# A hybrid decoder trunk on one core: HGRN's four heads in one tile, and fixed places for levels, outputs, splits and the compression

## The chip, the cores and the metric

The kernel runs on one core of one Trainium2 chip. The metric is the device time of one execution in microseconds, the median of repeated runs. The core's engines are TensorE (PE; its weight loads stand apart in the profile as PEld), the vector engine (DVE), the scalar engine (ACT), GpSimd (POOL) and the queue that issues the DMAs (SP). TensorE writes only to PSUM, which the kernel uses as eight banks of 128 x 512 float32.

## The reference

Two layers on 256 tokens of width 1024. Each layer, cut to what matters here:

```python
xn = rms_norm(h, norm_mix[l]);  proj = xn @ w_in[l]             # 3352 columns
# HGRN2: 4 heads of 128, chunks; per head, with b = cumsum(log f) inside a chunk
f = lb + (1 - lb) * sigmoid(f_logit);  k = 1 - f;  q = silu(q)
A = einsum(q, k, exp(b_t - b_s)), causal;  o = A v + (q exp(b)) S
S = exp(b_last) S + (k exp(b_last - b)) v
o_hg = rms_norm(o) * silu(g)
# NSA: 8 heads of 64 in 2 groups, gates over three branches
kc, vc = silu(blocks(k) + pe @ w1) @ w2                          # 15 compressed blocks
o_cmp = softmax(q kc) vc;  o_slc, o_swa: softmax attention over selected blocks and a window
h = h + concat(o_hg, o_nsa) @ w_out[l]
xn = rms_norm(h, norm_ffn[l])
h = h + (silu(xn @ w_gate) * (xn @ w_up)) @ w_ffn_out[l]         # 2816 wide
```

With 256 tokens all four blocks of 64 are selected and the window of 512 takes in every earlier token, so the kernel computes two full causal attentions (b = 0 and 1) beside the compressed one. All is float32.

## The kernel before

**Weights.** The matrices come in 204 units of at most 128 x 1024, in the order in which they are used, through four raw buffers. Each is split into a high half (`whi`, an ACTIVATE on the scalar engine, L143) and a low half (`wlo`, a subtraction on the vector engine, L144), with six buffers each. A dense product is then three TensorE products in float32r (`mm3`, L324, which keeps a list `products` of all of them); a plain float32 product shows as two instructions in the profile.

**Order.** A planner fixes the order of every engine's instructions at build, by priorities and by its own costs; on the chip each engine works through its queue in order, with semaphores between engines. `tc.high_priority(offset=...)` raises a priority, and `after(ins, others)` keeps `ins` behind `others` in that order without a wait of its own. `HOLD` and `PACE` say behind which of the `products` an instruction is held.

**A layer.** Norm and transposes of h (`norm_T`, two halves of 128 tokens); projections B, C and A for keys, values and queries; `gates(0)`, the forget gate and q of HGRN heads 0 and 1; the compression, whose hidden layer (`phid`, L510) works on four column tiles at once, is transposed (`phT`, L516), and ends in the normed and rotated key `kcb`, transposed as `pkT` (L551); `gates(1)`; then the attention scores and outputs, the projections `hi` and `hg` of HGRN (96 products in all, listed from `begin`) and HGRN's levels, which the planner interleaves.

**Attention outputs.** In `outputs(t)` a step turns four heads of probabilities in each of two groups g (`pPT`, L662), copies them to SBUF (`PT`, L666: scalar engine for g = 0, vector engine for g = 1), and multiplies them with the values (`pO`, L673), g = 0 and g = 1 on the two column tiles of 64. Two calls of two and four steps make six steps a layer. The products of one step are emitted behind the next step's transposes, but at a high priority that lets them go ahead.

**HGRN.** The decay is built up in levels. Blocks of one token (`pd`, L758), then levels 1 to 7 that double the block: at each level small products of K and Q (`pl`, L779 and L790) fill the off-diagonal part of the blocks, and the vector engine then multiplies Q by the forget product of the earlier half, K by that of the later half, and the two halves of the forget products with each other (L801, L802, L809). Levels up to 5 are merged into `blk` by a predicated copy (L814) and copied to `AT` by GpSimd; levels 6 and 7 are copied to `AT` by the scalar engine (L824). `p8` is the product across the two chunks of 128, copied to `A01` (L832). The head products `po` (L843, L844) take `AT`, `A01` and v. All of it works on two pairs of heads (hp = 0, 1), each with tiles of its own.

**Output projection and FFN's entry.** `wo_part` multiplies the mixed heads with w_out for one half t; `residual(0)`; while t = 1 is still multiplied, `norm_T(0)` makes the FFN's input for t = 0; `residual(1)`. The FFN's first column block is done per half (`ffn_in_tok`), so that `norm_T(1)` can come between them:

```python
        last, lo = norm_T(0, gain1, *X2[:2], "b", hold=begin + HOLD[2])
        for hh in range(2):
            held = units[U["fu", 0, hh]][6]
            if held is not None:
                after(held, lo)
        state["behind"] = [last]
        residual(1, py, lo)
...
        ffn_in_tok(0, 0)
        norm_T(1, gain1, *X2[:2], "b", hold=begin + HOLD[3])
        ffn_in_tok(0, 1)
```

Here `last` is the scalar engine's last copy of the normed half, `lo` are the vector engine's subtractions for its low half, and `units[...][6]` is the split's subtraction. GpSimd computes the reciprocal root of the norm in two operations (L339, L340), and the vector engine multiplies (`xn`, L343).

Of the kernel before, what the change touches and what calls it, by code (L numbers as in the profile page):

```python
# [42 lines left out]
LEV_PRIO, BLOCK_PRIO, PACE = 250, 3000, (0, 14)  # L43
HOLD, HOLD_C = (18, 18, 16, 36), 1
# [46 lines left out]
def trunk(ctx: ExitStack, tc: tile.TileContext, x, w_in, w_out, lbl, gnorm, q_gain, k_gain,  # L91
# [23 lines left out]
    state = {"loaded": 0, "split": 0}  # L115

# [16 lines left out]
    def split_to(n):  # L133
        while state["split"] < min(n, len(units)):
            load_to(state["split"] + 1)
            u = units[state["split"]]
            a, b = u[1], u[2]
            hi = wsp.tile([128, 1024], F32R, name="whi")
            lo = wsp.tile([128, 1024], F32R, name="wlo")
            u[4] = hi[:, : a * b].rearrange("p (a b) -> p a b", b=b)  # L140
            u[5] = lo[:, : a * b].rearrange("p (a b) -> p a b", b=b)
            with tc.high_priority(offset=SPLIT_PRIO):
                after(S.activation(u[4], u[3], AF.Copy), state.pop("behind", ()))  # L143
                u[6] = V.tensor_sub(u[5], u[3], u[4].bitcast(F32))  # L144
            state["split"] += 1
# [111 lines left out]
    AT = [one.tile([128, NT, 2, 128], F32, name=f"AT{hp}") for hp in range(2)]  # L257
    for hp in range(2):
        nc.gpsimd.memset(AT[hp], 0.0)
# [69 lines left out]
    def norm_T(t, gain, xh, xl, tag, behind=(), hold=None):  # L329

        with tc.high_priority():
            ss = sm.tile([128, 4], F32, name="n_ss")
            lo = []
# [7 lines left out]
            for c in range(2):  # L341
                cs = slice(512 * c, 512 * c + 512)
                V.scalar_tensor_tensor(xn[:, cs], h[:, t, cs], ss[:, 3:4], gain[c], op0=OP.mult, op1=OP.mult)  # L343
# [17 lines left out]
    for l in range(NL):  # L361
# [20 lines left out]
        HG, FB, last_sig = [], [], []  # L382

        def gates(hp):
# [3 lines left out]
            F = wk.tile([128, 2, T], F32, name="F", bufs=2)  # L388
            K = wk.tile([128, 2, T], F32, name="K", bufs=2)
# [8 lines left out]
            Q = wk.tile([128, 2, T], F32, name="Q", bufs=2)  # L398
# [3 lines left out]
            HG.append((F, K, Q))  # L402
            FB.append(wk.tile([128, 256], F32, name="FT", bufs=2))
# [97 lines left out]

        p = bank("phid", "e")[:, :256]
        for u in range(4):
            w = w1t[u]
            for jj in range(2):
                for kv in range(2):
                    for q in range(2):
                        j = 4 * u + 2 * jj + q
                        r0 = 64 * kv + 32 * q
                        PE.matmul(p[r0:r0 + 32], flat[:, kv, j], w[:, kv, 2 * jj + q],  # L510
                                  start=(j < 2), stop=(j >= 14))
# [3 lines left out]
        for c in range(2):  # L515
            PE.matmul(p[:, c], hid[:, 128 * c:128 * c + 128], C("sel"), start=True, stop=True)  # L516
# [26 lines left out]
        rk = rstd(kcs[:32], 1, 64, "kc_rs")  # L543
# [7 lines left out]
        PE.transpose(p[:, :32], kcb[:32].rearrange("p g d -> p (g d)"), ident[:32, :32])  # L551
# [100 lines left out]
        def outputs(t):  # L652
# [3 lines left out]
            def turned(b, sb):  # L656

                pts = []
                for g in range(2):
                    p = bank("pPT", "c")  # L660
                    for hg in range(4):
                        PE.transpose(p[:, 128 * hg:128 * hg + 128],  # L662
                                     P[t, g][:, hg, b, 128 * sb:128 * sb + 128], ident)
                    pt = turn[:, len(turns) % 4]
                    turns.append(pt)
                    pts.append((pt, V.tensor_copy(pt, p) if g else S.activation(pt, p, AF.Copy)))  # L666
                return pts

            def summed(b, sb, pts):

                with tc.high_priority(offset=BLOCK_PRIO):
                    for g in range(2):
                        m = PE.matmul(po[64 * g:64 * g + 64], vtok[:, b, sb, 64 * g:64 * g + 64], pts[g][0],  # L673
                                      start=(b == 0 and sb == 0), stop=False, skip_group_check=True)
                        after(m, [q[1] for q in pts])

            held = None
            for b, sb in steps:
                pts = turned(b, sb)
                if held is not None:  # L680
                    summed(*held)
# [66 lines left out]
        with tc.high_priority(offset=LEV_PRIO):  # L748
            A01, FT, blk, decays = [], [], [], []
            blocks = [(t, i, n) for t in range(NT) for i in range(2) for n in range(4)]  # L750
            for hp in range(2):
                F, K, Q = HG[hp]
                FT.append(F.rearrange("p h t -> p (h t)"))

                p = bank("pd", "b")[:, :128].rearrange("p (b s) -> p b s", s=32)
                for t, i, n in blocks:
                    ts = slice(128 * t + 32 * n, 128 * t + 32 * n + 32)
                    PE.matmul(p[32 * n:32 * n + 32, 2 * t + i], K[:, i, ts], Q[:, i, ts], start=True, stop=True)  # L758
                decays.append(V.tensor_mul(Q, Q, F))
                bl = wk.tile([128, 4, 32], F32, name="blk", bufs=2)  # L760
                blk.append(bl)
                V.tensor_mul(bl, p, C("ident32")[:, None, :].to_broadcast([128, 4, 32]))
            for lev in range(1, 8):
                half = 1 << (lev - 1)
                n4 = 256 // half

                pl = bank("pl", "b")
                if lev < 6:
                    pl = pl[:, :128].rearrange("p (g b c) -> p g b c", g=2, c=16)
                else:  # L770
                    pl = pl[:, :4 * half].rearrange("p (g c) -> p g c", g=2)
                last = None
                with tc.high_priority(offset=BLOCK_PRIO):
                    for hp in (1, 0):
                        F, K, QF = HG[hp]
                        if lev < 6:
                            for t, i, n in blocks:
                                ts = slice(128 * t + 32 * n, 128 * t + 32 * n + 32)
                                m = PE.matmul(pl[32 * n:32 * n + 32, hp, 2 * t + i], K[:, i, ts],  # L779
                                              QF[:, i, ts].rearrange("p (n c a) -> p n c a", c=2, a=half)[:, :, 1],  # L780
                                              start=True, stop=True)
                                after(m, [last] if last else [products[begin + PACE[0] + (lev - 1) * PACE[1]]] + decays)
                                last = m
                            continue
                        for t in range(NT):
                            for n in range(64 // half):
                                for i in range(2):
                                    s0 = 128 * t + 2 * half * n
                                    r0 = 64 * n + half * i
                                    m = PE.matmul(pl[r0:r0 + half, hp, half * t:half * t + half], K[:, i, s0:s0 + half],  # L790
                                                  QF[:, i, s0 + half:s0 + 2 * half], start=True, stop=True)
                                    after(m, [last] if last else decays)
                                    last = m
                decays = []
                for hp in range(2):
                    F, K, QF = HG[hp]
                    qv = QF.rearrange("p h (n c a) -> p (h n) c a", c=2, a=half)
                    kv = K.rearrange("p h (n c a) -> p (h n) c a", c=2, a=half)
                    fv = FT[hp].rearrange("p (n c) -> p n c", c=2)
                    if lev < 7:  # L800
                        V.tensor_mul(qv[:, :, 1], qv[:, :, 1], fv[:, :, 0:1].to_broadcast([128, n4, half]))  # L801
                        decays.append(V.tensor_mul(kv[:, :, 0], kv[:, :, 0], fv[:, :, 1:2].to_broadcast([128, n4, half])))  # L802
                    else:
                        f7 = FT[hp].rearrange("p (h t c) -> p h t c", t=NT, c=2)
                        V.tensor_mul(QF[:, :, 192:256], QF[:, :, 192:256], f7[:, :, 1, 0:1].to_broadcast([128, 2, 64]))
                        V.tensor_mul(K[:, :, 0:64], K[:, :, 0:64], f7[:, :, 0, 1:2].to_broadcast([128, 2, 64]))
                    if lev < 7:
                        f2 = (FB[hp] if lev % 2 else F.rearrange("p h t -> p (h t)"))[:, :n4]
                        V.tensor_mul(f2, fv[:, :, 0], fv[:, :, 1])  # L809
                        FT[hp] = f2  # L810
                    if lev < 6:
                        lm = lev_m[:, 16 * lev - 16:16 * lev]
                        dst = blk[hp].rearrange("p b (n c a) -> p b n c a", c=2, a=half)[:, :, :, 1]
                        V.copy_predicated(dst, lm[:, None, :].to_broadcast([128, 4, 16]).rearrange("p b (n a) -> p b n a", a=half),  # L814
                                          pl[:, hp].rearrange("p b (n a) -> p b n a", a=half))
# [227 lines left out]
```

## Time and profile before

| | us |
|---|---|
| median of 3 runs | 684.99 (684.43 to 685.22) |
| the profiled execution's own time | 685.0 |
| its span, first to last instruction | 683.1 |
| TensorE busy | 667.0 |
| vector engine busy | 469.7 |
| scalar engine busy | 379.6 |
| GpSimd busy | 30.1 |

The profiled execution's own time is its span and 1.9 us around it. Busy is the time in which an engine had at least one instruction in work; TensorE's products overlap, so the durations of single products add up to more than that. Starts are counted from the first instruction.

### The profile page before, as it was taken

Reading aid. Unit: us, or ns where it says so; the run is one execution under the profiler, and the core shown is the slowest. Engines: PE = TensorE matmul, PEld = TensorE weight load, DVE = VectorE, ACT = ScalarE, POOL = GpSimd, SP = SyncE. Lnnn points to the kernel's source line nnn. Section 1 sums busy time; section 2 is a strip of 40 time slices with the busy share of each in tenths; the row PEclk is TensorE's granted clock in tenths of the full one; section 3 lists DMA queues with packets and bytes.
Section 4 is the critical chain, followed back from the end, with each engine's and each line's share of the span. In section 5 each row is a group of like instructions: output and inputs, shape, how many; then the busy total and the mean of one; then the engine's idle time right before and its main releaser. Section 6 shows DMA issues by size and latency. Waiting matters only on the chain.

```text
span 683.1 us, 11845 instructions
## 1 busy us (share of the span) xinstructions
PE 667.0 (98%) x4607; PEld 554.6 (81%) x4607; DVE 469.7 (69%) x853; ACT 379.6 (56%) x676; POOL 30.1 (4%) x72
## 2 busy tenths in 40 slices
PE   6999999999999999999999999999999999999997
PEld 3869876688888888888878897658898888888886
DVE  4879999577665556666588979858685566665552
ACT  5536778636555555555466558656555555555550
POOL 2600001001000000000010000010000000000000
PEclk9999999999999999999999999999999999999999
DMA  7798541353765665666678632404376666665521
GB/s 253 246 335 266 169 107 51 100 178 121 248 187 187 190 192 194 194 185 185 196 230 286 203 110 64 125 1 154 94 229 203 188 187 190 197 191 187 185 93 62
DMA packets 86574, 118.90 MB, mean 174 GB/s; under 512 B 5035, under 2 KB 69365, under 8 KB 86518
## 3 DMA queue, kind: packets, MB, share of 16 engines
q1 hardware_dynamic: 86518, 118.15, 56.1%
q8 instruction: 36, 0.59, 0.4%
q14 instruction: 20, 0.16, 0.1%
HBM read 117.08 MB, written 1.05 MB: 173 GB/s over the span
## 4 chain that ended last, share of the span: by engine, by line
PE 80%; DVE 8%; DMA 4%; ACT 4%; issue 2%; POOL 1%; SPq 0%; POOLq 0%; DVEq 0%; ACTq 0%
PE pgu L929 22%; PE pz L327 17%; PE pgu L932 11%; PE pt L327 9%; PE py L327 5%; DMA wraw<-in_w_in_dram 4%; DVE wlo L144 3%; PE pO L673 2%; PE pgt L327 2%; ACT whi L143 2%; PE pPT L662 2%; PE pf L327 1%; PE pxn L346 1%; PE pl L779 1%; PE pq L327 1%
## 5 line engine op out<-in xcount | busy, mean ns | idle before, releaser
L144 DVE TENSOR_TENSOR wlo<-wraw,whi 128x1024 fp32r<-128x1024 f32 (+1 forms) x204 | 244.9, 1206 | 141.7 <-ACT whi L143 140.6
L143 ACT ACTIVATE whi<-wraw 128x1024 fp32r<-128x1024 f32 (+1 forms) x204 | 212.4, 1044 | 147.1 <-PE pgu L929 43.5
L929 PE MATMUL pgu<-x,whi 128*128 128x512 f32 x640 | 174.7, 394 | 0.0
L929 PEld LDWEIGHTS pgu<-x,whi 128*128 128x128 f32 x640 | 110.7, 189 | 15.7
L327 PE MATMUL pz<-whi,ahl 128*128 128x512 f32 x352 | 112.5, 391 | 0.0
L932 PEld LDWEIGHTS pgu<-x,wlo 128*128 128x128 f32 x640 | 98.1, 189 | 13.5
L932 PE MATMUL pgu<-x,wlo 128*128 128x256 f32 x640 | 101.7, 281 | 0.0
L327 PE MATMUL pt<-whi,x 128*128 128x512 f32 (+1 forms) x320 | 97.9, 383 | 0.0
L327 PEld LDWEIGHTS pz<-whi,ahl 128*128 128x128 f32 x352 | 65.9, 188 | 13.9 <-DVE ahl L946 0.5
L327 PE MATMUL pz<-wlo,ahl 128*128 128x512 f32 x176 | 68.9, 392 | 0.0
L327 PEld LDWEIGHTS pt<-whi,x 128*128 128x128 f32 x320 | 58.5, 191 | 10.3 <-DVE x L352 0.5
L327 PE MATMUL pt<-wlo,x 128*128 128x512 f32 (+1 forms) x160 | 61.6, 385 | 0.3 <-DVE wlo L144 0.3
L327 PE MATMUL py<-whi,x 128*128 128x512 f32 x128 | 42.0, 398 | 0.0
L327 PEld LDWEIGHTS pz<-wlo,ahl 128*128 128x128 f32 x176 | 33.0, 188 | 6.4
L327 PEld LDWEIGHTS pt<-wlo,x 128*128 128x128 f32 x160 | 30.6, 191 | 5.2 <-DVE wlo L144 0.7
L592 ACT ACTIVATE P<-pS,nm 128x128 f32<-128x128 f32 (+1 forms) x64 | 26.1, 424 | 6.3 <-DVE nm L639 5.0
L327 PEld LDWEIGHTS py<-whi,x 128*128 128x128 f32 x128 | 24.1, 188 | 4.7
L938 ACT ACTIVATE sl<-sl 128x512 f32<-128x512 f32 x20 | 12.7, 634 | 27.0 <-DVE sl L937 27.0
L327 PE MATMUL py<-wlo,x 128*128 128x512 f32 x64 | 25.1, 392 | 0.0
L327 PE MATMUL pf<-x,whi 128*128 128x256 f32 x128 | 23.8, 286 | 0.1
L327 PE MATMUL pgt<-whi,x 128*128 128x256 f32 x128 | 23.8, 285 | 0.0
L327 PE MATMUL pq<-x,whi 128*128 128x256 f32 x128 | 23.6, 284 | 0.0
(222 smaller groups left out, 829.4 us busy)
## 6 DMA issues: line engine op xcount, KB each, us to landing
wraw<-in_w_ffn_in_dram SPq DMA_DIRECT2D x88, 512.0 KB, 3.6
wraw<-in_w_in_dram SPq DMA_DIRECT2D x48, 512.0 KB, 5.3
wraw<-in_w_ffn_out_dram SPq DMA_DIRECT2D x44, 512.0 KB, 3.7
w<-in_cmp_w_k_dram SPq DMA_DIRECT2D x8, 512.0 KB, 4.7
w<-in_cmp_w_v_dram SPq DMA_DIRECT2D x8, 512.0 KB, 7.1
wraw<-in_w_out_dram SPq DMA_DIRECT2D x16, 256.0 KB, 4.1
wraw<-in_w_out_dram SPq DMA_DIRECT2D x8, 512.0 KB, 4.9
wraw<-in_w_in_dram SPq DMA_DIRECT2D x8, 280.0 KB, 5.3
```

Source lines behind the costliest of these rows:

```text
L143: after(S.activation(u[4], u[3], AF.Copy), state.pop("behind", ()))
L144: u[6] = V.tensor_sub(u[5], u[3], u[4].bitcast(F32))
L327: products.append(PE.matmul(o, a[u], b[v], start=start and i == 0, stop=stop and i == 2, skip_group_check=skip))
L346: tr = PE.transpose(p[:, 128 * k:128 * k + 128], xn[:, 512 * c + 128 * k:512 * c + 128 * k + 128], ident)
L592: e = S.activation(o, i, f, **kw)
L662: PE.transpose(p[:, 128 * hg:128 * hg + 128], P[t, g][:, hg, b, 128 * sb:128 * sb + 128], ident)
L673: m = PE.matmul(po[64 * g:64 * g + 64], vtok[:, b, sb, 64 * g:64 * g + 64], pts[g][0], start=(b == 0 and sb == 0), stop=False, skip_group_ ...
L779: m = PE.matmul(pl[32 * n:32 * n + 32, hp, 2 * t + i], K[:, i, ts], QF[:, i, ts].rearrange("p (n c a) -> p n c a", c=2, a=half)[:, :, 1], ...
L929: products.append(PE.matmul(pp[b], w[0][:, k, s], X[2][:, 4 * hh + k].rearrange("p c t -> p (c t)"), start=(hh == 0 and k == 0), stop=Fals ...
L932: products.append(PE.matmul(pp[b][:, T:], w[1][:, k, s], X[0][:, 4 * hh + k], start=False, stop=(hh == 1 and k == 3), skip_group_check=True))
L938: S.activation(sl, sl, AF.Silu)
```

## The change

HGRN's F, K and Q of all four heads are one tile each, and so are AT, A01, blk and FT: every level is one set of operations. The forget gate's scaling goes from the vector engine to the scalar engine. The diagonal blocks and each level are one chain of products, every level held behind a product of the projections (behind product 7 the first, then 14 further each, up to the 91st for level 7). An output's product for g = 0 stands behind the next step's transposes, that for g = 1 follows at a high priority. Compression: the hidden layer's products are one chain (in layer 1 in the order of units 3, 0, 1, 2), `phT` is held behind the 29th product of `gates(0)`, the key's reciprocal root is two GpSimd operations instead of twelve on the vector engine, and `pkT` is held behind the 8th product of `hi`. `norm_T` is cut in two: `normed` (squares, root, multiplication) and the transposes; for t = 1 `normed` is emitted right after the residual, and the weight splits around it are given fixed neighbours.

```diff
-LEV_PRIO, BLOCK_PRIO, PACE = 250, 3000, (0, 14)
-HOLD, HOLD_C = (18, 18, 16, 36), 1
+LEV_PRIO, BLOCK_PRIO, PACE = 250, 3000, (6, 14)
+HOLD, HOLD_C, HOLD_T = (18, 18, 16, 36), 1, 28
...
-                after(S.activation(u[4], u[3], AF.Copy), state.pop("behind", ()))
+                after(S.activation(u[4], u[3], AF.Copy), hi_behind.pop(0) if hi_behind else ())
                 u[6] = V.tensor_sub(u[5], u[3], u[4].bitcast(F32))
+                if lo_behind:
+                    after(u[6], lo_behind.pop(0))
+                    lo_held.append(u[6])
...
-    def norm_T(t, gain, xh, xl, tag, behind=(), hold=None):
+    def normed(t, gain, behind=()):
...
+        return xn, sq, m
+
+    def norm_T(t, gain, xh, xl, tag, behind=(), hold=None, xn=None):
+
+        if xn is None:
+            xn = normed(t, gain, behind)[0]
...
-                V.tensor_scalar(F[:, i], F[:, i], omlb[:, l, hd:hd + 1], lb[:, l, hd:hd + 1],
-                                op0=OP.mult, op1=OP.add)
+                S.activation(F[:, i], F[:, i], AF.Identity, scale=omlb[:, l, hd:hd + 1], bias=lb[:, l, hd:hd + 1])
...
+        order = (3, 0, 1, 2) if l else (0, 1, 2, 3)
+        behind = []
+        for u in order:
...
+                        with tc.high_priority(offset=BLOCK_PRIO if behind else 0):
+                            m = PE.matmul(p[r0:r0 + 32], flat[:, kv, j], w[:, kv, 2 * jj + q],
+                                          start=(u == order[0] and jj == 0), stop=(u == order[3] and jj == 1))
+                        after(m, behind)
+                        behind = [m]
...
+            m = PE.matmul(p[:, c], hid[:, 128 * c:128 * c + 128], C("sel"), start=True, stop=True)
+            after(m, [products[begin - 96 + HOLD_T]])
...
-        rk = rstd(kcs[:32], 1, 64, "kc_rs")
+        rk = sm.tile([128, 1], F32, name="kc_rs")[:32]
+        nc.gpsimd.tensor_scalar(kcs[:32], kcs[:32], 1.0 / 64, EPS, op0=OP.mult, op1=OP.add)
+        nc.gpsimd.tensor_tensor(rk, kcs[:32], mhalf[:32], op=OP.pow)
...
-            def summed(b, sb, pts):
-
-                with tc.high_priority(offset=BLOCK_PRIO):
-                    for g in range(2):
+            def summed(b, sb, pts, behind=[]):
+
+                for g in range(2):
+                    with tc.high_priority(offset=BLOCK_PRIO * g):
...
-                        after(m, [q[1] for q in pts])
+                        after(m, [q[1] for q in pts] + behind)
...
-                    summed(*held)
+                    summed(*held, behind=turned.last)
...
+        after(kT, [products[begin + 7]])
...
+                for hd in (3, 2, 1, 0):
+                    for t in range(NT):
+                        for n in range(4):
+                            m = PE.matmul(p[32 * n:32 * n + 32, 4 * t + hd], KH[:, hd, rows(t, n)],
+                                          QH[:, hd, rows(t, n)], start=True, stop=True)
+                            after(m, behind)
+                            behind = [m]
...
+                behind = [products[begin + min(PACE[0] + (lev - 1) * PACE[1], 95)], decay]
+                with tc.high_priority(offset=BLOCK_PRIO):
+                    for o, a, b in prods:
+                        m = PE.matmul(o, a, b, start=True, stop=True)
+                        after(m, behind)
+                        behind = [m]
...
+                    V.tensor_mul(qv[:, :, 1], qv[:, :, 1], fv[:, :, 0:1].to_broadcast([128, n4, half]))
+                    decay = V.tensor_mul(kv[:, :, 0], kv[:, :, 0], fv[:, :, 1:2].to_broadcast([128, n4, half]))
+                    FT = (FB if lev % 2 else FA)[:, :n4]
+                    V.tensor_mul(FT, fv[:, :, 0], fv[:, :, 1])
...
-        last, lo = norm_T(0, gain1, *X2[:2], "b", hold=begin + HOLD[2])
-        for hh in range(2):
-            held = units[U["fu", 0, hh]][6]
-            if held is not None:
-                after(held, lo)
-        state["behind"] = [last]
+        xn0, _, turn0 = normed(0, gain1)
+        last, lo = norm_T(0, gain1, *X2[:2], "b", hold=begin + HOLD[2], xn=xn0)
         residual(1, py, lo)
+        xn1, sq1, turn1 = normed(1, gain1)
+
+        for hh, ins in enumerate((turn0, res[-1])):
+            after(units[U["fu", 0, hh]][6], [ins])
+        hi_behind += [[last], [sq1]]
+        lo_behind += [[turn1], [turn1]]
...
-        norm_T(1, gain1, *X2[:2], "b", hold=begin + HOLD[3])
+        last, lo = norm_T(1, gain1, *X2[:2], "b", hold=begin + HOLD[3], xn=xn1)
+        after(lo_held.pop(), lo)
```

## Rows read from the trace of the kernel before

**Rows 1.** The page's first part, busy time and share of the span.
```profile
PE 667.0 (98%) x4607; PEld 554.6 (81%) x4607; DVE 469.7 (69%) x853; ACT 379.6 (56%) x676; POOL 30.1 (4%) x72
```
**Rows 2.** Waits, longest in total first: us in total, times, longest.
```profile
PE pxn L346 <- DVE xn L343: 6.0, 4, 4.2
...
PEld pO L673 <- DVE PT L666: 3.1, 9, 0.5
```
**Rows 3.** Windows: length, busy of PE, PEld, DVE, ACT, POOL, clock, DMA, GB/s.
```profile
30.00:45.00 15.00, 14.87 (x77) 12.61 (x77) 12.15 (x28) 6.95 (x12) 0.00 (x0) 1.00 1.04 341
...
411.50:433.00 21.50, 21.19 (x368) 15.79 (x368) 21.26 (x57) 17.40 (x60) 0.00 (x0) 1.00 0.42 99
```
**Rows 4.** Groups of TensorE's instructions by line: busy us, mean ns, idle before.
```profile
L673 PE MATMUL pO<-PT,vtok 128*64 128x512 f32 x48 | 17.5, 616 | 0.2
```
**Rows 5.** Timeline of TensorE in the attention outputs: start us, us, instruction, count.
```profile
113.47 1.08 PE L673 MATMUL pO<-PT,vtok 128*64 128x512 f32 x4
...
122.94 1.08 PE L662 MATMUL pPT<-cst,P 128*128 128x128 f32 x8
...
132.75 1.70 PE L673 MATMUL pO<-PT,vtok 128*64 128x512 f32 x4
...
435.52 1.79 PE L673 MATMUL pO<-PT,vtok 128*64 128x512 f32 x4
```
**Rows 6.** Timeline of TensorE in HGRN's levels, with idle time before in brackets.
```profile
86.02 0.74 PE L779 MATMUL pl<-Q,K 128*32 128x16 f32 x64
...
87.47 0.45 PE L779 MATMUL pl<-Q,K 128*32 128x16 f32 x32
...
89.18 0.46 PE L779 MATMUL pl<-Q,K 128*32 128x16 f32 x32
89.58 0.50 PE L327 MATMUL pt<-wlo,x 128*128 128x512 f32 x1
...
90.38 0.39 PE L327 MATMUL pt<-wlo,x 128*128 128x512 f32 x1
...
413.58 0.46 PE L758 MATMUL pd<-Q,K 128*32 128x32 f32 x32 [0.31 <-DVE Q L401]
```
**Rows 7.** Groups of the vector engine's instructions by line and form.
```profile
L801 DVE TENSOR_TENSOR Q<-Q,F 128x256 f32<-128x256 f32 x12 | 4.9, 422 | 1.8 <-PE pl L779 1.8
...
L393 DVE TENSOR_SCALAR F<-F,omlb,lb 128x256 f32<-128x256 f32 x8 | 3.2, 405 | 0.0
...
L759 DVE TENSOR_TENSOR Q<-Q,F 128x512 f32<-128x512 f32 x4 | 2.7, 676 | 0.0
```
**Rows 8.** Timeline of TensorE where the compressed key is transposed, layer 0.
```profile
72.80 0.28 PE L327 MATMUL pq<-x,whi 128*128 128x256 f32 x1
73.89 0.25 PE L551 MATMUL pkT<-cst,kcb 32*128 32x32 f32 x1 [0.81 <-DVE kcb L549]
```
**Rows 9.** Timelines of the vector engine and TensorE behind the hidden layer, layer 0.
```profile
49.14 1.22 DVE L144 TENSOR_TENSOR wlo<-wraw,whi 128x1024 fp32r<-128x1024 f32 x1
...
50.37 0.66 PE L516 MATMUL phT<-cst,hid 128*128 128x64 f32 x4 [0.47 <-ACT hid L513]
```
**Rows 10.** Timeline of all engines round FFN's norm, layer 0.
```profile
155.29 0.31 POOL L339 TENSOR_SCALAR n_ss<-n_ss 128x1 f32<-128x1 f32 x1 [44.53 <-ACT xn L337]
...
161.07 2.35 DVE L144 TENSOR_TENSOR wlo<-wraw,whi 128x1024 fp32r<-128x1024 f32 x2
...
162.47 1.12 POOL L339 TENSOR_SCALAR n_ss<-n_ss 128x1 f32<-128x1 f32 x1 [6.21 <-ACT xn L337]
...
165.15 0.63 PE L346 MATMUL pxn<-cst,xn 128*128 128x128 f32 x4 [0.72 <-DVE xn L343]
```
**Rows 11.** Timelines of TensorE and the scalar engine at HGRN's end, layer 0.
```profile
116.39 0.69 PE L790 MATMUL pl<-Q,K 128*64 128x64 f32 x16
...
122.31 0.39 PE L327 MATMUL pt<-whi,x 128*128 128x512 f32 x1
...
128.86 0.37 ACT L832 ACTIVATE A<-p 128x256 f32<-128x256 f32 x1
...
135.38 0.83 PE L844 MATMUL po<-vh,AT 128*128 128x128 f32 x6
```

More of the change, by code (lines that the diff above doesn't have):

```diff
@@ L255, in trunk @@
     tabc = one.tile([128, NL, 2, 64], F32, name="tabc")
-    AT = [one.tile([128, NT, 2, 128], F32, name=f"AT{hp}") for hp in range(2)]
-    for hp in range(2):
-        nc.gpsimd.memset(AT[hp], 0.0)
+    AT = one.tile([128, NT, 4, 128], F32, name="AT")
+    nc.gpsimd.memset(AT, 0.0)
     kB = one.tile([128, 2, 2, T], F32R, name="kB")
@@ L342, in norm_T @@
                 cs = slice(512 * c, 512 * c + 512)
-                V.scalar_tensor_tensor(xn[:, cs], h[:, t, cs], ss[:, 3:4], gain[c], op0=OP.mult, op1=OP.mult)
+                m = V.scalar_tensor_tensor(xn[:, cs], h[:, t, cs], ss[:, 3:4], gain[c], op0=OP.mult, op1=OP.mult)
+        return xn, sq, m
+    def norm_T(t, gain, xh, xl, tag, behind=(), hold=None, xn=None):
+        if xn is None:
+            xn = normed(t, gain, behind)[0]
+        lo = []
+        with tc.high_priority():
+            for c in range(2):
                 p = bank("pxn", tag)
@@ L499, in trunk @@
         gates(0)
+        begin = len(products)
         p = bank("phid", "e")[:, :256]
-        for u in range(4):
+        order = (3, 0, 1, 2) if l else (0, 1, 2, 3)
+        behind = []
+        for u in order:
             w = w1t[u]
@@ L748, in trunk @@
         with tc.high_priority(offset=LEV_PRIO):
[L749 to L762, printed above, removed]
+            rows = lambda t, n: slice(128 * t + 32 * n, 128 * t + 32 * n + 32)
@@ new lines, in trunk @@
+            p = bank("pd", "b")[:, :256].rearrange("p (b s) -> p b s", s=32)
+            behind = []
+            with tc.high_priority(offset=BLOCK_PRIO):
[6 more added lines that the diff above has]
+                            behind = [m]
@@ L772, in trunk @@
[L772 to L793, printed above, removed]
@@ L826, in trunk @@
-            for hp in range(2):
-                F, K, QF = HG[hp]
-                p = bank("p8", "b")[:, :256].rearrange("p (h s) -> p h s", s=128)
-                for i in range(2):
-                    PE.matmul(p[:, i], K[:, i, 0:128], QF[:, i, 128:256], start=True, stop=True)
-                a01 = wk.tile([128, 2, 128], F32, name="A01", bufs=2)
-                S.activation(a01, p, AF.Copy)
-                A01.append(a01)
+                prods = []
+                for t in range(NT):
+                    for hd in range(4):
+                        if lev < 6:
+                            p = pl[:, :128].rearrange("p (b c) -> p b c", c=16)
+                            prods += [(p[32 * n:32 * n + 32, 4 * t + hd], KH[:, hd, rows(t, n)],
+                                       QH[:, hd, rows(t, n)].rearrange("p (n c a) -> p n c a", c=2, a=half)[:, :, 1])
+                                      for n in range(4)]
+                            continue
+                        p = pl[:, :4 * half].rearrange("p (t h a) -> p t h a", t=NT, a=half)
+                        for n in range(64 // half):
+                            s0, r0 = 128 * t + 2 * half * n, 64 * n + half * (hd % 2)
+                            prods.append((p[r0:r0 + half, t, hd // 2], KH[:, hd, s0:s0 + half],
+                                          QH[:, hd, s0 + half:s0 + 2 * half]))
@@ new lines, in trunk @@
+                for n in range(64 // half):
+                    for i in range(2):
+                        r0, s0 = 64 * n + half * i, 2 * half * n
+                        S.activation(AT[s0:s0 + half, :, i::2, s0 + half:s0 + 2 * half],
+                                     pl[r0:r0 + half, :4 * half].rearrange("p (t h a) -> p t h a", t=NT, a=half), AF.Copy)
+            p = bank("p8", "b").rearrange("p (h s) -> p h s", s=128)
+            for hd in range(4):
+                PE.matmul(p[:, hd], KH[:, hd, 0:128], QH[:, hd, 128:256], start=True, stop=True)
```

90 lines of the change are left out of this document (39 added, 51 removed).

## Prediction

> **What bounds the kernel now.** I read the page's shares of busy time first. TensorE is busy for 98% of the span [rows 1]: the time is its queue, and an edit pays only if that queue gets shorter or waits less. The table of waits comes next: of what TensorE's products waited for, one line is large, and most of it lies at the start, which the change leaves alone [rows 2]. So the gain must be sought where waits hide inside "busy": a product that has begun counts as busy while its partner in another column tile still waits for its operand. The table shows these as waits of weight loads: nine of them, for the vector engine's copies of transposed probabilities [rows 2].
>
> Then the windows by stage. From 30 to 45 us DMA is saturated: here weights set the time, and TensorE can gain nothing [rows 3]. In layer 1's attention and HGRN stage the vector engine is busy 21.26 of 21.50 us [rows 3]: whatever TensorE takes from it there comes late. The FFN, half of the span, is one unbroken stream that the change doesn't touch except at its entry. The place to look at is therefore, in each layer, the stretch from the gates to the FFN's first products.
>
> **Attention outputs.** Each of the 12 steps has two products (g=0 and g=1) on different column tiles, recorded as four. Where both copies had landed, all four start together and last 1.08 us; where g=1's copy was late, up to 1.79 [rows 5]. All 12 take 17.5 us [rows 4], against 12 x 1.08 = 13.0: 4.5 us are waits in disguise. The change puts the products behind the next step's eight transposes, which last 1.08 us [rows 5] and give a late copy the time that it lacks (at most 1.79 - 1.08 = 0.71). The last step of each call has no transposes behind which to stand: 113.47 was free anyway, 132.75 lost 0.62 [rows 5], and taking as much for its like in layer 1, 1.2 us stay. That leaves 3.3. Against it, the second bank that these transposes need comes from a ring of three, so they may now wait for the scalar engine's copy instead. I take -3.0; bounds -3.3 and 0.
>
> **HGRN in one tile.** The number of products is the same. What falls away is groups: the diagonal blocks went in two groups of 32 per layer, and one level of layer 0 and one of layer 1 was also split. Two halves take 0.45 + 0.46 us, one whole 0.74 [rows 6]; a projection product right behind a group takes 0.50 instead of 0.39 [rows 6]. So a merge is worth 0.17 + 0.11 = 0.28, and four of them -1.1 us (bound 0, if a group that has to wait for all four heads starts later).
>
> On the vector engine two multiplications of 0.422 become one of 0.676 [rows 7], so each of six levels gets 0.34 us shorter; the forget gate's eight TENSOR_SCALARs of 0.405 move to the scalar engine as ACTIVATEs of Identity, where I price them by the same duration: 1.6 us a layer, in a stage in which that engine has room. In a window where the vector engine is full this brings copies and scalings forward. It is worth at least the wait of 0.31 before the second group of diagonal blocks [rows 6]: -0.3 (bounds -1.6, what the moved TENSOR_SCALARs take in one layer, and 0).
>
> **Compression.** The transpose pkT began 1.09 us after the product before it, and TensorE was idle for 0.81 of that [rows 8]. It now stands behind eight products of the next projection, and its reciprocal root runs as two GpSimd operations instead of twelve on the vector engine. Behind it in TensorE's queue now stand more projection products, which depend on nothing of it. Alone among products of another kind it costs some 0.1 more, as the product behind a group does [rows 6]. I take 0.81 - 0.11, so -0.7 (bounds -0.8 and 0).
>
> The hidden layer's products are chained, and phT waits until 29 products of the gates are through. In layer 0 phT sat idle for 0.47 [rows 9], but the low half of the gates' first weights was only finished at 49.14 + 1.22 = 50.36 [rows 9], and the third product needs it: the wait for phT hides the wait for that unit. Take away one and the other is late next. Worth 0 (bounds -0.5 and +0.2).
>
> **Splits round FFN's norm.** The second row half's transposes wait 0.72 us for xn in layer 0 [rows 10], and its like in layer 1 much the same (all such waits but the start's 4.2 make 1.8 [rows 2]). Two weight splits of 2.35 us together stand between the residual and xn on the vector engine, and GpSimd's first operation of the norm, 0.31 us with the vector engine idle, takes 1.12 beside them [rows 10]. The change moves one split ahead of the residual and the later ones behind xn; the other stays. The moved half of the norm issues two squares, two GpSimd operations and two multiplications and no DMA. If GpSimd gets its 0.31 back, xn comes 0.8 earlier and the wait is gone; if the split ahead delays the lows and the residual as much as it saves, nothing is won. Between -1.4 and 0 for two layers I take -1.0, nearer the first, since the squares too stand ahead of a split now.
>
> The Trainium skill speaks against more here: "SBUF — State Buffer", section "SBUF: two separate sides", says that a VectorE operation with two SBUF inputs and a GpSimd operation that reads SBUF lock each other out, and that whoever comes second is blocked outright. The trace agrees (0.31 beside 1.12). By that rule the split that stays could block GpSimd as before, this term would be 0, and the sum would give 680.9.
>
> **New waits.** The order on every engine is fixed at build; some of what is freed will come back elsewhere. The three waits named (0.81, 0.47, 0.31) make 1.6 us; I put two thirds of that on the other side: +1.0 (bounds 0 and +3.0).
>
> **Sum.** -3.0 - 1.1 - 0.3 - 0.7 + 0 - 1.0 + 1.0 = -5.1. From the profiled execution's own 685.0 us that gives 679.9; the median is 684.99, so nothing has to be converted.
>
> **The rivals.**
>
> *The pairs keep their price.* The transposes that now stand ahead need banks that the late copies free, so the lag moves from the product to the transpose. For it speaks that the ring has three banks and a step takes two; against it, that the lag is at most 0.71 and eight transposes last longer. Without that term: 682.9.
>
> *It doesn't bind.* The holds are only lower bounds in an order worked out beforehand; if the planner already put the products about there, or the vector engine's lateness simply hits the next instruction in the queue, the stage lasts as long as before: 685.0, give or take 1.4 (0.2%, about what a measurement of this kernel can tell from no change). For it speaks the full vector engine [rows 3].
>
> *HGRN's tail is late (slower).* Level 7 ran at 116.39 [rows 11]; it is now pinned behind product 91 of 96, and with the last at 122.31 [rows 11] that is about 121.3: 4.9 us later. Behind it come the cross-chunk product, its copy (which ended at 128.86 + 0.37 = 129.2 [rows 11]), the head products, HGRN's norm and the transposes before the output projection. Most of the head products ran at 135.38 [rows 11], behind the attention outputs, so 6.2 us of slack stand against 4.9. It decides once the copies of levels 6 and 7 sit over 1.3 us longer in the scalar engine's queue; each microsecond beyond costs one in each layer, since nothing else of the output projection is then left to do. To turn -5.1 into a loss it must be over 2.6 us late in both; at 4 us: 685.0 - 5.1 + 8.0 = 687.9.
>
> **Chances.** The forecast, with its terms within their bounds (676 to 682): 0.53. The pairs keep their price (682 to 683.6): 0.20. No effect that can be told (683.6 to 686.4): 0.15. Slower: 0.12. So faster 0.73, same 0.15, slower 0.12. All best bounds together make -3.3 - 1.1 - 1.6 - 0.8 - 0.5 - 1.4 = -8.7, or 676.3; I set the low end at 676.0, and the high end in the middle of the third case, 685.5: 0.8 of the chances lie between. The likeliest case's own range is 676 to 682.
>
> **What would show it.** Right: the outputs' 12 groups near 1.1 us each (13 to 14 us in all, four of them possibly longer); the diagonal blocks in one group of 64; no idle time before pkT; the FFN norm's wait under 0.3; the vector engine some 8 to 10 us less busy in all. Wrong: the waits of the pPT transposes for copies grow by what the products lose (first rival); idle time before the head products or the transposes of HGRN's output (third rival); or the stretch from the gates to the FFN as long as before with waits under new names. The prediction is wrong above all if layer 0's early stage, which DMA bounds, swallows more than the term that I left at nothing, or if the new order meets a late copy at a place that no row here shows.

## The result and the profile after

Before 685.11 us (median of 4 runs, 684.43 to 685.59), after 678.06 us (4 runs, 677.17 to 678.12): ratio 0.9895, 95% interval 0.9878 to 0.9912. That is 7.05 us less, 1.0%; 5.1 were forecast. The profiled execution after took 677.17 us, with a span of 675.4.

The page's first part after, beside [rows 1]:

```profile
PE 660.5 (98%) x4607; PEld 551.5 (82%) x4607; DVE 462.4 (68%) x767; ACT 379.3 (56%) x670; POOL 30.1 (4%) x67
```

TensorE has the same 4607 instructions and still 98%: what went was mostly time inside "busy", 6.5 of the span's 7.7 us. The table of waits after (columns as in [rows 2]):

```profile
PE pxn L357 <- DVE xn L345: 4.5, 2, 4.2
...
PE pf L330 <- DVE wlo L145: 1.1, 1, 1.1
PE pkc L541 <- DVE hk L537: 1.0, 1, 1.0
PE pS L638 <- DVE kB L587: 1.0, 2, 0.5
PE pPT L678 <- ACT PT L682: 0.6, 2, 0.3
...
PEld pO L690 <- DVE PT L682: 0.8, 4, 0.2
```

Of the weight loads' nine waits for the vector engine's copies of PT, 3.1 us [rows 2], four are left, 0.8 us. The norm's waits fell from four to two. Three waits have new names: pf (the forget gate's projection) for the low half of its weights, pkc (the compressed key and value) for hk (the hidden layer's activation), and pS (the scores) for kB (the low half of the keys).

The outputs, by group (beside [rows 4]) and in TensorE's timeline of layer 0 (beside [rows 5]):

```profile
L690 PE MATMUL pO<-PT,vtok 128*64 128x512 f32 x48 | 13.8, 613 | 0.0
```

```profile
111.57 0.66 PE L678 MATMUL pPT<-cst,P 128*128 128x128 f32 x4 [0.29 <-ACT PT L682]
112.16 1.43 PE L690 MATMUL pO<-PT,vtok 128*64 128x512 f32 x4
...
115.83 1.08 PE L690 MATMUL pO<-PT,vtok 128*64 128x512 f32 x4
...
127.71 1.38 PE L690 MATMUL pO<-PT,vtok 128*64 128x512 f32 x4
...
132.31 1.94 PE L690 MATMUL pO<-PT,vtok 128*64 128x512 f32 x8
```

17.5 us became 13.8, and the last two steps run back to back at 0.97 each.

FFN's norm, second row half, layer 0 (beside [rows 10]):

```profile
159.35 1.21 DVE L145 TENSOR_TENSOR wlo<-wraw,whi 128x1024 fp32r<-128x1024 f32 x1
...
160.31 0.42 POOL L341 TENSOR_SCALAR n_ss<-n_ss 128x1 f32<-128x1 f32 x1 [5.85 <-ACT xn L339]
...
162.46 0.60 PE L357 MATMUL pxn<-cst,xn 128*128 128x128 f32 x4
```

No idle time stands before the transposes any more. Adding up on the timelines, for each product, the time from its start to the next start shows where the gain lies: 3.9 us at the output products, 0.87 in each layer at FFN's first products (the wait for xn), 1.0 at the scores. The compression and the gates (pf, and pq for HGRN's q) give and take: hidden layer -1.7, pq -1.6, pf +2.5. Counted from behind the first loads, layer 0 is 2.55 us shorter up to its first large FFN product and 0.4 in its FFN; layer 1's stage up to the same product is 4.70 shorter.

### The profile page after: what moved, and what is told of

It reads as the page before. It is cut to its first block, busy times and chain, and to the rows that moved or that the text cites. A ratio compares the mean times of both kernels' runs of the same rounds, so it can differ in the third digit from the quotient of the medians.

```text
span 675.4 us, 11740 instructions
## 1 busy us (share of the span) xinstructions
PE 660.5 (98%) x4607; PEld 551.5 (82%) x4607; DVE 462.4 (68%) x767; ACT 379.3 (56%) x670; POOL 30.1 (4%) x67
## 4 chain that ended last, share of the span: by engine, by line
PE 86%; DVE 4%; ACT 4%; DMA 4%; issue 1%; POOL 0%; SPq 0%; DVEq 0%; ACTq 0%; POOLq 0%
PE pgu L941 22%; PE pz L330 17%; PE pgu L944 11%; PE pt L330 10%; PE py L330 7%; DMA wraw<-in_w_in_dram 4%; PE pgt L330 3%; PE pq L330 3%; PE pf L330 2%; PE pO L690 2%; PE pPT L678 1%; DVE wlo L145 1%; ACT whi L144 1%; PE pl L806 1%; PE pxn L357 1%
## 5 line engine op out<-in xcount | busy, mean ns | idle before, releaser
L948 ACT ACTIVATE sl<-pgu 128x256 f32<-128x256 f32 x40 | 15.0, 374 | 15.0 <-PE pgu L944 15.0
```

Of the source, the lines that this page charges most:

```text
L948: S.activation(sl[:, b], pp[b][:, T:], AF.Copy)
```

## The experiments

Each ran beside the kernel before on its own chip, so ratios to that kernel are compared; 0.001 is 0.69 us. Intervals are +-0.0012 to +-0.0022, so neighbours that differ by 0.002 are not told apart by time alone. A ratio can differ from the quotient of the two medians by up to 0.0008. Profiled executions also differ by up to 1.7 us in the first loads' wait, which belongs to no part.

| kernel | median us | ratio | 95% interval |
|---|---|---|---|
| change, again | 678.49 | 0.9896 | 0.9876 to 0.9915 |
| outputs undone | 682.35 | 0.9946 | 0.9934 to 0.9959 |
| outputs alone | 681.10 | 0.9934 | 0.9919 to 0.9948 |
| FFN's norm undone | 681.49 | 0.9936 | 0.9921 to 0.9951 |
| HGRN undone | 687.83 | 1.0023 | 1.0011 to 1.0035 |
| HGRN alone | 684.24 | 0.9967 | 0.9956 to 0.9979 |
| outputs and FFN alone | 679.36 | 0.9896 | 0.9878 to 0.9914 |
| compression undone | 677.94 | 0.9881 | 0.9862 to 0.9899 |
| hidden layer undone | 678.21 | 0.9881 | 0.9861 to 0.9901 |
| HGRN and key undone | 677.22 | 0.9877 | 0.9855 to 0.9898 |
| HGRN and key's hold undone | 678.41 | 0.9893 | 0.9877 to 0.9910 |
| chain in layer 1 only | 677.49 | 0.9876 | 0.9855 to 0.9898 |

**Outputs undone, outputs alone.**

```diff
-                for g in range(2):
-                    with tc.high_priority(offset=BLOCK_PRIO * g):
+                with tc.high_priority(offset=BLOCK_PRIO):
+                    for g in range(2):
...
-                        after(m, [q[1] for q in pts] + behind)
+                        after(m, [q[1] for q in pts])
```

> The changed kernel with the attention outputs as before: each step's two products stand where they stood, not behind the next step's transposes; all else stays changed. Theory 'pairs': between the two traces the time from the starts of the output products to the next starts fell by 3.9 us (20.6 to 16.8), and that is the hold. Expected: 678.1 + 3.9 = 682.0 us, at least +3; the 12 groups again some 17 us in all. Rival 'relief': the copies came early because HGRN in one tile takes work from the vector engine, and the hold does nothing: 678.1 + 0 to 1 us, and the groups stay near 13 us.

> The kernel before with the change of the attention outputs alone. Theory 'pairs': 685.1 - 3.9 = 681.2 us. Rival 'relief': without the lighter vector engine the lag moves to the transposes: 684 us or more, and TensorE's pPT rows show waits for copies that sum to over 2 us.

Undoing costs 0.0050 against the change (3.4 us, give or take 1.6), alone it gives 0.0066 (4.5 us, give or take 1.0). With the outputs undone, the group and the waits of the whole kernel, and last the group with the outputs alone:

```profile
L689 PE MATMUL pO<-PT,vtok 128*64 128x512 f32 x48 | 17.2, 618 | 0.0
```

```profile
PE pPT L678 <- ACT PT L682: 0.6, 2, 0.3
...
PEld pO L689 <- DVE PT L682: 2.8, 8, 0.6
```

```profile
L674 PE MATMUL pO<-PT,vtok 128*64 128x512 f32 x48 | 13.4, 614 | 0.0
```

With the hold gone, eight waits for copies, 2.8 us, stand here although HGRN is still in one tile; with the hold alone the group takes 13.4 us although HGRN is in two. The transposes' wait of 0.6 stands with the outputs undone as well, so it isn't the hold's price. "Pairs" holds, "relief" falls.

**FFN's norm undone.** Norm and splits as in the kernel before: the norm isn't cut off from its transposes, and no split is held behind xn.

```diff
-        xn0, _, turn0 = normed(0, gain1)
-        last, lo = norm_T(0, gain1, *X2[:2], "b", hold=begin + HOLD[2], xn=xn0)
+        last, lo = norm_T(0, gain1, *X2[:2], "b", hold=begin + HOLD[2])
...
-        hi_behind += [[last], [sq1]]
-        lo_behind += [[turn1], [turn1]]
```

> The changed kernel with FFN's norm and the splits round it as before. Theory 'splits': the first FFN products' time to the next start fell by 0.87 us in each layer between the traces, which is the wait for xn: 678.1 + 1.75 = 679.9 us, GpSimd's first operation of the second half's norm again near 1.1 us. Rival: the wait went because the residual came earlier for other reasons: 678.1, give or take 0.4.

It costs 0.0040 (2.7 us) where 1.75 were expected, a difference that the interval hardly tells apart. Timeline of this kernel at the same place and, last, at the FFN's second multiplication slt (silu of the gate times up, for t = 1) in layer 0:

```profile
159.86 2.35 DVE L144 TENSOR_TENSOR wlo<-wraw,whi 128x1024 fp32r<-128x1024 f32 x2
...
161.25 1.12 POOL L338 TENSOR_SCALAR n_ss<-n_ss 128x1 f32<-128x1 f32 x1 [6.21 <-ACT xn L336]
...
163.94 0.63 PE L345 MATMUL pxn<-cst,xn 128*128 128x128 f32 x4 [0.74 <-DVE xn L342]
...
173.52 2.47 DVE L144 TENSOR_TENSOR wlo<-wraw,whi 128x1024 fp32r<-128x1024 f32 x2 [1.60 <-ACT whi L143]
173.66 1.06 ACT L143 ACTIVATE whi<-wraw 128x1024 fp32r<-128x1024 f32 x1 [0.18 <-DMA wraw<-in_w_ffn_out_dram]
...
175.90 0.42 DVE L960 TENSOR_TENSOR slt<-slt,pgt 128x256 f32<-128x256 f32 x1
...
176.37 0.44 PE L963 MATMUL pgT<-cst,slt 128*128 128x128 f32 x2 [0.95 <-DVE slt L960]
```

The 0.74 is back in layer 0 and its like (0.73) in layer 1, and later in layer 0 a further 0.95: two splits stand ahead of slt on the vector engine. Layer 0's large FFN products take 1.1 us more than in the change's trace, which with 2 x 0.87 makes the 2.7, about. But the 1.1 isn't shown to be the order's price: the kernel before has two splits ahead of the same slt and no idle time there, and the change's own second profile waits 0.36 there.

The 0.42 of the change is the same blocking as before, shorter. Beside a split GpSimd's operation ended 0.16 to 0.17 us after the split in all 56 cases of the fourteen traces, whether it took 0.42, 0.72, 0.88 or 1.12; alone it took 0.29 to 0.31. The Trainium skill's "SBUF — State Buffer", section "SBUF: two separate sides", says that of a vector operation with two SBUF inputs and a GpSimd operation that reads SBUF, the one that starts second is blocked until the other ends. The gain of 0.87 came from what stands ahead of GpSimd's operation: one split, begun 0.96 us earlier, instead of two.

**HGRN undone, HGRN alone, outputs and FFN alone.** HGRN undone restores the two tiles of two heads, with PACE (0, 14):

```diff
-        FH, KH, QH = [wk.tile([128, 4, T], F32, name=n) for n in "FKQ"]
+            F = wk.tile([128, 2, T], F32, name="F", bufs=2)
...
-                S.activation(F[:, i], F[:, i], AF.Identity, scale=omlb[:, l, hd:hd + 1], bias=lb[:, l, hd:hd + 1])
+                V.tensor_scalar(F[:, i], F[:, i], omlb[:, l, hd:hd + 1], lb[:, l, hd:hd + 1],
+                                op0=OP.mult, op1=OP.add)
...
```

> The changed kernel with HGRN in two tiles of two heads, with its gates, levels and their places as before; the rest stays changed. Forecast by my terms (merged groups 1.1, relief 0.3): 678.1 + 1.4 = 679.5 us. Rival 'merges are worth nothing': the time of the levels' products did not fall between the two traces (8.94 and 9.06 us), so 678.1, give or take 0.4. Rival 'relief': over +3 us, since the output pairs, the scores and the compression become late again.

> The kernel before with HGRN of four heads in one tile (gates, levels, their places) and nothing else of the change. My terms (merged groups 1.1, relief 0.3): 1.4 us less than the kernel before, ratio 0.998. Rival 'HGRN carries the change': the run with HGRN undone lost all 7 us and more, so HGRN alone gives 5 us or more, ratio 0.993 or less. Rival 'worth nothing alone': ratio 1.000, give or take 0.001.

> The kernel before with the outputs and FFN's norm and splits changed, HGRN and compression as before. Theory 'collision': HGRN in two tiles was slow only beside the compression's holds, where the vector-gate products of the next projection waited 2.1 us in each layer for the copies of their banks. Then this kernel gains what the two parts cost when undone, 3.5 + 2.8 us: ratio 0.991, and that wait is absent. Rival 'HGRN is needed': the two parts give nothing without it: ratio 1.000 to 1.003, and the wait of 2 us stands here too.

HGRN undone was slower than even the kernel before: 0.0127 above the change, 8.7 us. Only "relief" (over +3) allowed for that, and its mechanism shows in part: the scores come late (84.77 against 82.64 in the change), but the output pairs don't become as late as before (six waits for copies, 1.3 us). One wait is new and large, that of the projection hg for a bank that still holds HGRN's v, until the scalar engine copies it to vh. The wait and the timeline of layer 0:

```profile
PE pt L331 <- ACT vh L764: 4.3, 2, 2.1
```

```profile
79.59 0.24 PE L572 MATMUL pkT<-cst,kcb 32*128 32x32 f32 x1
...
84.77 0.39 PE L643 MATMUL pS<-cab,idb 128*128 128x512 bf16 x1
...
99.28 1.27 ACT L671 ACTIVATE P<-P,cf 128x128 f32<-128x128 f32 x4
100.45 1.07 ACT L764 ACTIVATE vh<-pt 128x512 f32<-128x512 f32 x2
...
101.09 0.50 PE L331 MATMUL pt<-whi,x 128*128 128x512 f32 x1 [2.15 <-ACT vh L764]
```

TensorE stood still until the scalar engine, behind exponentials, scalings and splits, emptied a bank; the two `vh` copies came last of all. But HGRN alone gives only 0.0033 (2.3 us), and outputs and FFN without it 0.0104, as much as the whole change. So the one tile isn't needed for the gain, and the theory became "collision": two tiles are slow only beside the compression's holds.

**Which hold collides.** To the kernel with HGRN undone:

```diff
-        rk = sm.tile([128, 1], F32, name="kc_rs")[:32]
-        nc.gpsimd.tensor_scalar(kcs[:32], kcs[:32], 1.0 / 64, EPS, op0=OP.mult, op1=OP.add)
-        nc.gpsimd.tensor_tensor(rk, kcs[:32], mhalf[:32], op=OP.pow)
+        rk = rstd(kcs[:32], 1, 64, "kc_rs")
...
-        after(kT, [products[begin + 7]])
```

The first run took both edits, the second only the last line.

> The kernel with HGRN in two tiles that lost 7 us and more (HGRN alone undone), with one thing more undone: the compressed key's transpose has no hold and its reciprocal root is on the vector engine again. The hidden layer's chain and hold stay. Theory 'key': the hold on the transpose makes the kB split and so the scores late (they began at 84.8 us, 5.7 later than before), and the scalar engine, full with their exponentials, is late with the copies of the next projection: ratio 0.990 and no wait of 2 us for these copies. Rival 'hidden layer': its chain and hold make the key late: ratio 1.000 to 1.003 and the wait stays.

> The kernel with HGRN in two tiles that lost 7 us and more, with the hold on the compressed key's transpose alone undone: the reciprocal root stays on GpSimd, the hidden layer's chain and hold stay. Theory 'hold': the transpose waits in TensorE's queue for eight products of the next projection although the key is done, and that alone makes the scores late: ratio 0.988, no wait of 2 us for the copies of the next projection. Rival 'root': GpSimd's root, beside the splits of the vector engine, makes the key late: ratio 1.000 to 1.003, and the wait stays.

Both gain as the change does: 0.9877 and 0.9893. One line that holds one transpose back makes the difference between 1.0023 and 0.9893. The timeline with that line alone taken out, and last the change's own at the same place:

```profile
72.48 0.24 PE L572 MATMUL pkT<-cst,kcb 32*128 32x32 f32 x1
...
78.14 0.39 PE L643 MATMUL pS<-cab,idb 128*128 128x512 bf16 x1 [0.48 <-DVE kB L592]
...
91.27 0.61 ACT L764 ACTIVATE vh<-pt 128x512 f32<-128x512 f32 x1
91.75 1.08 ACT L144 ACTIVATE whi<-wraw 128x1024 fp32r<-128x1024 f32 x1
92.70 1.29 ACT L671 ACTIVATE P<-P,cf 128x128 f32<-128x128 f32 x4
```

```profile
95.80 0.58 ACT L759 ACTIVATE vh<-pt 128x512 f32<-128x512 f32 x1
...
96.02 0.91 PE L330 MATMUL pt<-whi,x 128*128 128x512 f32 x2
```

The key's transpose runs 7.1 us earlier, the scores 6.6, and TensorE doesn't wait for vh. It isn't lateness alone, though: the line also changes the order that the planner fixes on the scalar engine. With the hold, the first copy of vh stands behind four splits and the four scalings (99.28); without it, ahead of all eight. It came 9.2 us earlier: 3.9 because the exponentials begin earlier (82.86 against 86.80), the rest because it is no longer behind the eight. In the change itself there was no room either: the first copy stands behind three splits there and lands at 96.38, and the first product of hg starts at 96.43 (two products take 0.91 us there, elsewhere 0.62). With the root undone as well, the scores began at 82.75, about as late as in the change (82.64), but in layer 0 the copy stood ahead of the splits and landed at 92.24. How much of the lost time goes to lateness and how much to the new order, no run parts. Of the 8.9 us, the stalls explain 4.3 and a fallen clock behind the first of them (last section) some 1.4: the same 81 products took 6.29 us behind the first stall and 4.89 behind the second. The rest is spread over both layers' projections and scores and wasn't traced further.

**Compression undone, hidden layer undone, chain in layer 1 only.** From the change:

```diff
-        order = (3, 0, 1, 2) if l else (0, 1, 2, 3)
...
-                        after(m, behind)
-                        behind = [m]
...
-            after(m, [products[begin - 96 + HOLD_T]])
```

This is "hidden layer undone"; "compression undone" also takes back the root and pkT's hold; the last kernel is that one, with order, chain and HOLD_T kept `if l`.

> The changed kernel with the compression as before: the hidden layer's products neither chained nor reordered, no hold on its transposes or on that of the compressed key, the reciprocal root on the vector engine. My term: 0.7 us more than the changed kernel (ratio 0.9905 against the kernel before). By the traces' rows: 1.7 for the hidden layer's products and 0.8 for the idle time before pkT, less the new waits of 1.0 for hk and 0.7 for kB: +0.8, at most +2.5. Rival 'nothing': the new waits eat it, 0.9895.

> The changed kernel with the hidden layer's products neither chained nor reordered and their transposes without a hold; the compressed key's hold and its root on GpSimd stay. My term: 0 (ratio 0.9895 against the kernel before; bounds -0.2 to +0.5 us). Rival 'chain': the products' time to the next starts fell by 1.7 us between the traces; less the new wait of 1.0 for hk that the later transposes bring, +0.7 us or more, 0.9905.

> The changed kernel with the compression as before, except that the hidden layer's chain, order and hold stay in layer 1. By the stretches from the experiments' traces: without the whole compression part layer 0 is 1.2 us shorter (leaving out its first loads) and layer 1 is 0.4 longer; the chain alone is worth 0.8 in layer 1. So 1.2 + 0.4 = 1.6 us less than the changed kernel: ratio 0.987. Rival: the holds depend on each other, and layer 1 gets nothing from the chain without the key's hold: 0.988.

> The changed kernel itself once more, as a measure for the two others of this group on the same chip: ratio 0.9895 against the kernel before, as at first.

Undoing all or half of it made nothing slower: 0.9881 both, against 0.9895 and 0.9896 of the change. The 0.9905 expected of the whole part, and of the hidden layer by the rival 'chain', is outside both intervals; a gain isn't clear of the noise. The change's timelines in layer 0 show the price:

```profile
44.73 3.66 PE L521 MATMUL phid<-w,flat 128*32 128x256 f32 x64
...
50.07 0.39 PE L330 MATMUL pf<-x,wlo 128*128 128x256 f32 x1 [1.13 <-DVE wlo L145]
...
61.44 0.55 PE L529 MATMUL phT<-cst,hid 128*128 128x64 f32 x4
...
63.94 1.06 ACT L144 ACTIVATE whi<-wraw 128x1024 fp32r<-128x1024 f32 x1 [0.72 <-DMA wraw<-in_w_in_dram]
64.90 0.26 ACT L532 ACTIVATE hsg<-phT 128x128 f32<-128x128 f32 x1
65.03 1.23 DVE L145 TENSOR_TENSOR wlo<-wraw,whi 128x1024 fp32r<-128x1024 f32 x1 [0.45 <-ACT whi L144]
66.18 0.28 DVE L537 TENSOR_TENSOR hk<-hsg,phT 128x128 f32<-128x128 f32 x1
...
66.51 0.43 PE L541 MATMUL pkc<-w,hk 128*128 128x64 f32 x2 [1.00 <-DVE hk L537]
```

The transposes moved from 50.37 [rows 9] to 61.44, behind all 96 products of the gates, not 29. There their sigmoid hsg queues on the scalar engine behind a split whose weights land late, then hk on the vector engine behind the low half of the same split (65.03), and TensorE waits 1.00 for hk.

The last kernel, 0.9876, has the lowest ratio of those with one tile, its median 1.0 us under the change on the same chip (4 runs from 676.34 to 677.70 against 6 from 677.52 to 680.18). In the profiles its layer 1 is 1.2 us shorter than in the change's first profile and 1.9 shorter than in its second, so the change's own two profiles differ there by about as much as the parts that I meant to add up. A version that clearly beats the change isn't shown, only that this part needn't be there.

## Why the prediction was right, and where it was not

The sign, the range and the largest term held, and "it doesn't bind" is out: 7.05 us against the 1.4 that it allowed. What failed was how the parts add up.

*Outputs, -3.0.* Right in mechanism, under-sized: 3.4 us undone, 4.5 alone, 3.9 by the traces, against a best bound of 3.3. The groups came out at 13.8 in all, as named. The 1.2 us left for the last steps of the calls were mostly recovered (1.94 for two). That all four products start together was read too simply: the two of a pair do, and their second halves follow 0.48 us later; the sum doesn't use it. The rival "the pairs keep their price" is refuted: the transposes' wait is 0.6 with and without the hold.

*HGRN, -1.1 for merges and -0.3 for relief.* The sum is near (2.3 us alone; 1.0 on top of outputs and FFN, 0.9896 to 0.9881, which is within the intervals), the split is not. With HGRN alone, the levels' and diagonal blocks' groups of products take 11.5 us on TensorE instead of 11.9: 0.4, where four merges at 0.17 were to save 0.7. The outputs, however, fell from 17.5 to 16.4 there, which the outputs' hold would have taken anyhow. Whether that is relief of the vector engine or the planner's new order, the run doesn't part, and the remaining 0.8 wasn't traced. The vector engine is 7.3 us less busy, not 8 to 10. The moved forget-gate operations were priced at the vector engine's 0.405 us; on the scalar engine they take 0.594.

```profile
L404 ACT ACTIVATE F<-F,lb,omlb 128x256 f32<-128x256 f32 x8 | 4.5, 594 | 0.1
```

*HGRN's tail, the slower rival.* Refuted: level 7 did run later, but the head products came before the outputs of the second call, 12.6 us earlier than in [rows 11]:

```profile
119.58 0.69 PE L806 MATMUL pl<-Q,K 128*64 128x64 f32 x16
...
122.82 1.06 PE L851 MATMUL po<-vh,AT 128*128 128x128 f32 x8
```

*Compression, -0.7.* The step that failed. The idle time before pkT did go, and the wait for the unit's low half took phT's place, as written (1.13). But I priced the holds' own cost at 0.1, by the nearest rows; the runs show that the part as a whole gives nothing and may cost 1 us. I also took the hidden layer's chain and the hold on phT as worth 0, with a bound of +0.2, without asking what stands around them on the other engines: the wait for the low half is 1.13 where phT's was 0.47, and the wait for hk adds 1.00.

*FFN's norm, -1.0.* Right in mechanism, under-sized: 2.7 undone, 2.6 on top of the outputs (0.9934 to 0.9896). 1.75 is the wait in the two layers together, beyond the best bound of 1.4, which counted idle time alone; 1.1 stands at a place that I hadn't costed, the second multiplication slt, and may not belong to this part at all. The blocking by which the term would be 0 did happen: the split that stayed held GpSimd up. But it had begun 0.96 us before, so only 0.12 us was lost (0.42 against 0.30 alone).

*New waits, +1.0.* Near in size: pf, pkc and pS took 2.8 us of new or longer waits (1.1 + 1.0 + 0.7), against 1.6 that went: +1.2 net, but nearly all of it belongs to the compression.

Built up from the kernel before, the parts read: outputs -4.5 (0.9934), FFN's norm -2.6 more (0.9896), HGRN -1.0 more (0.9881), compression +1.0 (0.9896), -7.1 in all; the last two are within the intervals. So outputs and FFN gave 3.1 us more than their terms, and HGRN, compression and new waits together 1.1 less than theirs. That 679.9 came within 2 us of the result is in part luck: the second error hid a third of the first.

## What to carry to other kernels

Look for waits inside "busy": paired products in two column tiles hid 3.7 us, and a hold behind work that must be done anyway recovered them. Price a hold by everything behind it in every in-order queue, and look at what it does to the order on the other engines, since a planner lays that out anew. Test it with its neighbours both in and out: one line cost 9 us beside two tiles, while beside the one tile it and the root made no difference that could be measured (0.9881 with and without them, the hidden layer undone in both). A part that removes a named wait isn't a gain until the run without it is slower.

## What the runs showed of the hardware

With HGRN undone, the same stall of 2.15 us came in both layers. Windows of one microsecond each (columns as in [rows 3]), behind the first and behind the second, and a group of 64 level products behind each:

```profile
102.00:103.00 1.00, 1.00 (x5) 0.79 (x4) 1.00 (x4) 0.16 (x1) 0.00 (x0) 0.75 1.00 336
103.00:104.00 1.00, 1.00 (x4) 0.67 (x2) 0.84 (x5) 0.26 (x1) 0.00 (x0) 0.50 0.98 377
104.00:105.00 1.00, 1.00 (x42) 0.53 (x44) 0.00 (x0) 0.00 (x0) 0.00 (x0) 0.50 0.46 184
...
437.00:438.00 1.00, 1.00 (x39) 0.61 (x40) 0.96 (x5) 0.38 (x1) 0.00 (x0) 1.00 1.01 406
```

```profile
104.47 1.06 PE L802 MATMUL pl<-Q,K 128*32 128x16 f32 x64
...
437.70 0.74 PE L802 MATMUL pl<-Q,K 128*32 128x16 f32 x64
```

Behind the first the granted clock fell to 0.50 (1.2 instead of 2.4 GHz) for some 3 us, and the group took 1.06 us instead of 0.74; behind the second it stayed at 1.00. A stall can cost more than its length, and a stall of the same length doesn't always; what made the difference between these two stays open. The forget gate's ACTIVATE with a scale and a bias per partition took 0.594 us for 128x256, where the scalar engine's plain copy of that size out of PSUM took 0.37 [rows 11]. The Trainium skill's "ScalarE: Activation LUTs", section "What ACT_TABLE_LOAD costs", has a price for it: 186 ns, 0.833 ns per element and 93 ns for each of the two operands, an estimate of 0.585 us, which the trace bears out.
